# A two-layer hybrid backbone with routed experts: where a branch of the general path stands, and how rows and gates of the experts are made

## The chip, the cores and the metric

The kernel runs on one core of one Trainium2 chip. The time is the device time of one execution in microseconds (us). The core has five engines: TensorE (PE), VectorE (DVE), ScalarE (ACT), GpSimd (POOL) and SyncE (SP), each with its own stream of instructions, and 16 DMA engines that all queues share.

## The reference, cut to what matters

Two layers run over 256 latent tokens and 256 context tokens of width 1024. Each has an input projection, three groups of heads (retention, windowed and global attention), an output projection, and then a mixture of 16 experts of which each token uses two. The second layer needs only the latent tokens, so its experts see 256 rows, and those of the first see 512. Everything is f32.

```python
def _route(h, w_router, b_router):
    s = jax.nn.sigmoid(jnp.dot(h, w_router).astype(jnp.float32))
    ...
    w = jnp.take_along_axis(s, e_idx, axis=1)
    return e_idx, w / jnp.sum(w, axis=-1, keepdims=True)

def expert_block(args):
    xb, e = args
    a, u = jnp.split(xb @ w_gu[e], 2, axis=-1)
    return (jax.nn.silu(a) * u) @ w_down[e]

def reference(x, c, ctx, c_ctx, ada_w, ada_b, norm1, norm2, w_in, w_out, ret_decay, win_qk_gain, win_sink,
              glb_qk_gain, w_router, b_router, w_gate_up, w_down):
    for i in range(DEPTH):
        ...
        hx = _modulate(_rms(x, norm2[i]), sh2, s2).reshape(b * l, d)
        if last:
            x = x + g2 * _moe(hx, w_router, b_router, w_gate_up[i], w_down[i]).reshape(b, l, d)
        else:
            ...
            y = _moe(jnp.concatenate([hx, hc], 0), w_router, b_router, w_gate_up[i], w_down[i])
            x = x + g2 * y[:b * l].reshape(b, l, d)
            ctx = ctx + g2c * y[b * l:].reshape(ctx.shape)
    return x
```

`_modulate(h, shift, scale)` is h * (1 + scale) + shift. An expert has 8 MB of gate and up weights and 4 MB of down weights; two layers of 16 make 384 MB, which are read once.

## The kernel before, in words

**Stream of weights.** SP issues the weights in the order of their use as transfers of 1 MB into pages (`pump`, L164): per expert eight pieces of `w_gate_up` and four of `w_down`. A piece goes when a page is free; at most eight are in flight, since transfer n waits for the landing of transfer n - 8. In front of the experts the pages can be filled for expert 0 only, twelve pieces, because the experts run in an order that the routing finds (the fullest first): `order` holds it, and for each expert from 1 on SP loads its number from there into a register (`expert`, L144). The scheduler puts these loads together with the place where the code asks for them.

**Routing.** `route` turns the logits into probabilities, picks the two experts of each token, counts (a product with a triangular matrix, L1101 to L1106) and ranks the experts (L1120 to L1128, `order`). It works on small tiles of DVE, 30 or so instructions in a row. Meanwhile `rows` (L1013 to L1035) makes the normalized rows: factor and shift (L1016, L1017, L1019) and SP writes them to a buffer in DRAM, HX (L1020). In layer 1 it also cuts the rows into three bf16 parts `x3` (L1027 to L1035), on two pages of their own.

**An expert's rows.** `index` compares positions with a row of numbers: a one-hot matrix, in bf16, whose product with the token numbers (L1183) gives the row index of each slot; `gates` is a second product, of the same one-hot with the gates in three bf16 parts (L1194), which POOL has made (L1164 to L1169). In layer 0 POOL then gathers the rows from HX by an indirect transfer (L1213) and PE transposes them (`flip`, L1281). In layer 1 nothing is gathered: PE multiplies the rows' three parts with the one-hot (`place`, L1232, and L1249 in `pick_up`).

**An expert's products.** An expert with many tokens ("big": those with even numbers and 15 in layer 0; 0, 14 and 15 in layer 1) is computed as three products of high and low halves (L200 to L202); ACT makes the high half `hi` of each weight page (L190) and DVE the low one `lo` (L192), in five shared buffers. A small one (up to 64 tokens) multiplies in plain f32 (L1300, L1316). At an expert's end POOL scatters its result to DRAM (L1368). `between` puts the work on the next expert's rows between a running expert's pages.

**The general path.** If an expert gets more tokens than its slots hold, `overflow` (L1373) computes the rest in loops, behind a branch `tc.If(n > 0)` (L1388); with these inputs n is 0 and the branch jumps over it. All engines cross this branch. It stands in `moe` (L1436) just ahead of the first expert's rows, before the first weights behind expert 0's. Buffers that the general path uses too (those of `hi` and `lo`, lanes of the weight transfers) carry waits on both ways through the branch.

**What sets the order.** A scheduler orders the instructions of each engine by the order of the code and by dependencies; `issue_after` holds some work behind a named instruction.

Of the kernel before, what the change touches and what calls it, by code (L numbers as in the profile page):

```python
# [9 lines left out]
F32 = mybir.dt.float32  # L10
F32R = mybir.dt.float32r
BF = mybir.dt.bfloat16
# [9 lines left out]
NE = 16  # L22
# [38 lines left out]
class Kernel:  # L61
# [199 lines left out]
    def late_consts(self):  # L261
# [73 lines left out]
        self.tok = cp.tile([128, 4, 2], BF, name="tok")  # L335
        g.iota(self.tok[:, :, 0], pattern=[[128, 4]], base=-BIG, channel_multiplier=0, allow_small_or_imprecise_dtypes=True)
        g.iota(self.tok[:, :, 1], pattern=[[0, 4]], base=0, channel_multiplier=1, allow_small_or_imprecise_dtypes=True)
        self.tok2 = cp.tile([128, 4, 2], BF, name="tok2")
        v.tensor_scalar(self.tok2, self.tok, 2.0, None, op0=OP.mult)
# [568 lines left out]
    def out_proj(self, l):  # L908
# [27 lines left out]
        xr = [xg[t // 2][1][:, (t % 2) * 1024:(t % 2) * 1024 + 1024] for t in range(nt)]  # L936
        ss = self.tiny("ss2", [128, 4, 2])
# [51 lines left out]
        if nt == 4:  # L989
            mg.append(self.pgs.get("mods"))  # L990
            mb = mg[1][1]
            for r in range(2):
                self.modrow(mb[:, r * 1024:(r + 1) * 1024], l, r, 3, nc.gpsimd)
            self.spare += 1
            self.pump()
# [16 lines left out]
        def rows():  # L1012
            for t in range(nt):  # L1013
                b = mb[:, (t // 2) * 1024:(t // 2) * 1024 + 1024]
                if t % 2 and not l:
                    nc.scalar.activation(xr[t], xr[t], AF.Copy, scale=rs[:, t:t + 1])  # L1016
                    nc.gpsimd.tensor_tensor(xr[t], xr[t], b, op=OP.add)  # L1017
                else:
                    v.scalar_tensor_tensor(xr[t], xr[t], rs[:, t:t + 1], b, op0=OP.mult, op1=OP.add)  # L1019
                nc.sync.dma_start(self.HX[l][t * 128:(t + 1) * 128, :], xr[t])  # L1020
            if l:

                self.hx = [self.pgs.get("hx") for _ in range(2)]
                x3 = self.x3 = [self.hx[i // 2][1][:, (i % 2) * 1024:(i % 2) * 1024 + 1024].bitcast(BF).rearrange("p (t n) -> p t n", t=2)
                                for i in range(3)]
# [686 lines left out]
```

## Time and profile before

| | us |
|---|---|
| three runs | 1637.36, 1642.13, 1642.26 |
| median | 1642.13 |
| the profiled execution | 1637.78 |
| its span in the trace | 1635.5 |
| PE busy | 1443.6 (88%) |
| DVE busy | 884.2 (54%) |
| ACT busy | 612.8 (37%) |
| POOL busy | 200.6 (12%) |

The profile shows one execution, whose own time lies near the lowest of the three runs. Busy shares are means over very different stages: projections and attention, in which PE and DVE do small work and the transfer queues are half idle, the routing, in which nearly everything waits for a chain of small DVE instructions, and the experts, in which 384 MB go by. So the profile is read by windows of time, and in each window by what waits for what. Layer 0's routing lies at 331 to 361 us of the span, its experts behind it to some 800; layer 1's routing at 1099 to 1125, its experts to the end.

### The profile page before, as it was taken

What the parts mean: (1) busy time and instruction counts of PE and PEld (TensorE: products, weight loads), DVE (VectorE), ACT (ScalarE), POOL (GpSimd) and SP (SyncE); (2) the same over time, 40 slices, a digit from 0 to 9 for tenths busy, and PEclk for the clock granted to TensorE, in tenths of its full rate; (3) what the DMA queues carried; (4) which work ended last, traced back from release to release, by engine and by line L of the source; (5) the groups of instructions that cost most, each with busy time, mean ns of one, the idle gap of its engine ahead of it and who ended that gap; (6) DMA issues with size and microseconds to landing.
All of it is one profiled execution on the core that took longest, in us unless ns stands there. A gap on an engine that the chain in (4) does not pass through costs nothing. (4 is left out here: it accounts for less than half of the span.)

```text
span 1635.5 us, 21821 instructions
## 1 busy us (share of the span) xinstructions
PE 1443.6 (88%) x7890; PEld 864.6 (53%) x7890; DVE 884.2 (54%) x1648; ACT 612.8 (37%) x920; POOL 200.6 (12%) x216
## 2 busy tenths in 40 slices
PE   5999999929999999989888799976999888888888
PEld 4767756716664654645657667644433222222446
DVE  5776576476674654744779687967410000000577
ACT  3353404225563553643655554434300000000445
POOL 2000000440110110110033400021000000000030
PEclk9999999959999999999999999986999999999998
DMA  9763679538999999999997542743999999999993
GB/s 273 289 221 132 255 271 347 180 123 343 404 404 413 410 394 407 392 407 383 350 363 234 181 155 84 265 175 138 388 414 411 413 416 412 413 416 414 414 357 129
DMA packets 131099, 514.83 MB, mean 315 GB/s; under 512 B 14291, under 2 KB 40563, under 8 KB 92706
## 3 DMA queue, kind: packets, MB, share of 16 engines
q1 hardware_dynamic: 117536, 488.67, 76.3%
q0 software_dynamic: 8080, 16.60, 3.5%
q10 hardware_dynamic: 5362, 8.03, 1.5%
q8 instruction: 66, 1.08, 0.3%
q14 instruction: 55, 0.45, 0.1%
HBM read 503.24 MB, written 16.70 MB: 318 GB/s over the span
## 5 line engine op out<-in xcount | busy, mean ns | idle before, releaser
L192 DVE TENSOR_TENSOR lo<-w,hi 128x1024 fp32r<-128x1024 f32 x342 | 441.2, 1301 | 103.8 <-ACT hi L190 31.8
L190 ACT ACTIVATE hi<-w 128x1024 fp32r<-128x1024 f32 x344 | 359.4, 1059 | 179.9 <-PE gu L202 55.6
L1300 PE MATMUL gs<-w,ex 128*64 128x512 f32 x1280 | 298.9, 601 | 27.6 <-DMA w<-in_w_gate_up_dram 27.3
L1300 PEld LDWEIGHTS gs<-w,ex 128*64 128x64 f32 x1280 | 82.0, 136 | 196.5 <-issue 119.0
L201 PE MATMUL gu<-lo,ex 128*128 128x512 f32 (+1 forms) x384 | 155.7, 406 | 12.0 <-DVE lo L192 12.0
L1316 PE MATMUL ds<-w,ex 128*64 128x512 f32 x640 | 152.3, 603 | 7.9 <-DMA w<-in_w_down_dram 7.9
L202 PE MATMUL gu<-hi,ex 128*128 128x512 f32 (+1 forms) x384 | 153.5, 400 | 0.0
L200 PE MATMUL gu<-hi,ex 128*128 128x512 f32 (+1 forms) x384 | 134.5, 407 | 7.8 <-ACT hi L190 7.7
L1306 DVE TENSOR_TENSOR ex<-ex,gs 128x512 f32<-128x512 f32 x20 | 13.7, 687 | 214.6 <-PE gs L1300 214.6
L200 PE MATMUL px<-hi,hT 128*128 128x512 f32 (+1 forms) x304 | 114.6, 382 | 1.4 <-ACT hm L512 1.0
L201 PE MATMUL px<-lo,hT 128*128 128x512 f32 (+1 forms) x304 | 114.8, 378 | 0.4 <-DVE lo L192 0.4
L202 PE MATMUL px<-hi,hT 128*128 128x512 f32 (+1 forms) x304 | 114.3, 377 | 0.0
L1305 ACT ACTIVATE ex<-gs 128x512 f32<-128x512 f32 x20 | 11.9, 597 | 272.6 <-PE gs L1300 272.6
L1368 POOL DMA_INDIRECT y<-ex,ridx x28 | 43.7, 1561 | 568.5 <-ACT ex L1320 363.9
L201 PEld LDWEIGHTS gu<-lo,ex 128*128 128x128 f32 (+1 forms) x384 | 71.5, 186 | 39.5 <-DVE lo L192 21.5
L201 PE MATMUL dn<-lo,ex 128*128 128x512 f32 (+3 forms) x224 | 83.6, 374 | 5.6 <-DVE lo L192 5.6
L200 PEld LDWEIGHTS gu<-hi,ex 128*128 128x128 f32 (+1 forms) x384 | 70.4, 186 | 32.1 <-ACT hi L190 15.5
L1316 PEld LDWEIGHTS ds<-w,ex 128*64 128x64 f32 x640 | 40.0, 136 | 83.5 <-issue 56.8
L202 PE MATMUL dn<-hi,ex 128*128 128x512 f32 (+3 forms) x224 | 81.3, 364 | 0.0
L202 PEld LDWEIGHTS gu<-hi,ex 128*128 128x128 f32 (+1 forms) x384 | 71.5, 186 | 16.8 <-issue 0.2
L200 PE MATMUL dn<-hi,ex 128*128 128x512 f32 (+3 forms) x224 | 73.7, 370 | 0.0
L97 DVE COPY ex<-pl 128x512 f32<-128x512 f32 x12 | 8.3, 692 | 114.2 <-PE pl L1249 114.2
(344 smaller groups left out, 1945.1 us busy)
## 6 DMA issues: line engine op xcount, KB each, us to landing
w<-in_w_gate_up_dram SPq DMA_DIRECT2D x256, 1024.0 KB
w<-in_w_down_dram SPq DMA_DIRECT2D x128, 1024.0 KB
w<-in_ada_w_dram SPq DMA_DIRECT2D x40, 1024.0 KB
w<-in_w_in_dram SPq DMA_DIRECT2D x20, 1024.0 KB
w<-in_ada_w_dram SPq DMA_DIRECT2D x16, 512.0 KB
w<-in_w_out_dram SPq DMA_DIRECT2D x8, 1024.0 KB
y<-zero POOLq DMA_DIRECT2D x3, 1024.0 KB, 10.9
g<-modd ACTq DMA_DIRECT2D x6, 512.0 KB
```

What stands on the lines that cost most here:

```text
L97: nc.vector.tensor_copy(out, in_)
L190: nc.scalar.activation(hi, w, AF.Copy)
L192: (nc.gpsimd if after else nc.vector).tensor_tensor(lo, w, hi.bitcast(F32), op=OP.subtract)
L200: mm(o, a[0], b[0], start=first, stop=False)
L201: mm(o, a[0], b[1], start=False, stop=False)
L202: mm(o, a[1], b[0], start=False, stop=last)
L1300: nc.tensor.matmul(ps[n // 2][(n % 2) * 64:(n % 2) * 64 + 64], x[:, self.part(k)], t[:, n * 512:(n + 1) * 512], start=k == 0, stop=k == 7)
L1305: nc.scalar.activation(h, ps[0], AF.Silu)
L1306: nc.vector.tensor_tensor(h, h, ps[1], op=OP.mult)
L1316: nc.tensor.matmul(p[n * 64:n * 64 + 64], self.sx[2][:, self.part(ff)], t[:, f * 1024 + n * 512:f * 1024 + n * 512 + 512], start=ff == 0, ...
L1368: self.nc.gpsimd.indirect_dma_start(out=dst, out_offset=bass.IndirectOffsetOnAxis(ap=idx, axis=0), in_=y, in_offset=None, bounds_check=n - ...
```

## The change

Four things are changed together.

- `overflow(l)` is called behind `expert_down(l, 7)`, where it stood ahead of expert 0.
- One-hots are f32, and one product gives row index and gate (`ve` holds token number and gate side by side); `gates` and the three-part gates of POOL go. `arranged` sorts by one large multiplication on DVE, and gates come from DVE ahead of the ranking.
- In layer 1 the rows stay f32: `place` takes 16 f32 products where 48 bf16 ones stood, the two pages of parts are not taken, and the pages of the rows are kept to the end of the experts.
- In layer 0 HX is filled with the shift rows ahead of time by two transfers of 1 MB on ACT's queue, ACT scales the rows (four times), and POOL adds them into HX by accumulating transfers.

```diff
@@ norm and logits
+        if nt == 4:
+            for r in range(2):
+                nc.scalar.dma_start(self.HX[l][r * 256:(r + 1) * 256, :],
+                                    self.modd[l, r, 3 * 1024:4 * 1024].partition_broadcast(256))
...
         def rows():
             for t in range(nt):
-                b = mb[:, (t // 2) * 1024:(t // 2) * 1024 + 1024]
-                if t % 2 and not l:
+                if l:
+                    v.scalar_tensor_tensor(xr[t], xr[t], rs[:, t:t + 1], mb, op0=OP.mult, op1=OP.add)
+                    nc.sync.dma_start(self.HX[l][t * 128:(t + 1) * 128, :], xr[t])
+                else:
                     nc.scalar.activation(xr[t], xr[t], AF.Copy, scale=rs[:, t:t + 1])
-                    nc.gpsimd.tensor_tensor(xr[t], xr[t], b, op=OP.add)
-                else:
-                    v.scalar_tensor_tensor(xr[t], xr[t], rs[:, t:t + 1], b, op0=OP.mult, op1=OP.add)
-                nc.sync.dma_start(self.HX[l][t * 128:(t + 1) * 128, :], xr[t])
-            if l:
-                self.hx = [self.pgs.get("hx") for _ in range(2)]
...
-                for t in range(nt):
-                    nc.scalar.activation(x3[0][:, t], xr[t], AF.Copy)
-                for t, rest in enumerate((ma, mb)):
-                    nc.gpsimd.tensor_tensor(rest, xr[t], x3[0][:, t], op=OP.subtract)
-                    nc.scalar.activation(x3[1][:, t], rest, AF.Copy)
+                    nc.gpsimd.dma_start(self.HX[l][t * 128:(t + 1) * 128, :], xr[t], accum_op=OP.add)
...
@@ route
+        v.tensor_tensor(kw, s, sel, op=OP.mult)
+        v.tensor_reduce(gd, kw, axis=AX.X, op=OP.add)
+        v.reciprocal(gd, gd)
+        v.tensor_tensor(kx, kw, gd[:, :, None].to_broadcast([128, nt, 16]), op=OP.mult)
+        v.tensor_copy(ve[:, :, 0, 1], kx[:, :, 0])
...
-        def arranged(dst, src, e=v):
-            for t in range(nt):
...
-                e.tensor_tensor(m, perm, src[:, t, None, :].to_broadcast(b16), op=OP.mult)
-                v.tensor_reduce(dst[:, t], m, axis=AX.X, op=OP.add)
+        def arranged(dst, src):
...
+            v.tensor_tensor(m, perm[:, None].to_broadcast(o), src[:, :, None, :].to_broadcast(o), op=OP.mult)
+            v.tensor_reduce(dst, m, axis=AX.X, op=OP.add)
...
@@ index
         for t in range(nt):
-            nc.tensor.matmul(p[:, 0:2], oh[:, t], (self.tok2 if folded else self.tok)[:, t], start=t == 0, stop=t == nt - 1)
+            nc.tensor.matmul(p[:, 0:2], oh[:, t], ve[:, t], start=t == 0, stop=t == nt - 1)
+        self.placed = nc.vector.tensor_scalar(idx, p[:, 0:1], self.halfc[:S] if folded else float(BIG), None, op0=OP.add)
+        nc.vector.tensor_copy(gate, p[:, 1:2])
...
@@ place
-        for i in parts:
-            x = self.x3[i]
-            for t in range(nt):
-                for f in range(4):
+        for t in range(nt):
+            for f in range(4):
...
@@ moe
             self.expert_load(l, 0)
-            self.overflow(l)
...
             self.expert_down(l, e)
+            if e == NE // 2 - 1:
+                self.overflow(l)
```

How it moves instructions is seen at three places. The first is SP in front of layer 1's experts, from the read of `over1` to the first weight behind expert 0's (`w` is a weight page, `order1` the order of the experts, the row with eight waits the end of the jump). Before:

```order
L1377 TENSOR_LOAD over1_9940 [waits DVE_49]
L1388 COMPARE_AND_BRANCH
...
L1388 UNCONDITIONAL_BRANCH [waits DMAHW0_49,DMAHW1_49,DMAHW2_49,DMAHW3_49,DMAHW4_49,DMAHW5_49,DMAHW6_49,DMAHW7_49]
L1377 ISA x2
L164 ISA
L164 DMA w_10400<-in_w_gate_up_dram 128x2048 [waits DMAHW0_49,Activation_49]
L144 TENSOR_LOAD order1_9922
```

Eight loads of `order1` stand ahead of these rows. In the change, from the writes of HX on:

```order
L1020 DMA hx1_74<-xr_9511 128x1024 [waits DMAHW4_49,DVE_49]
L1020 DMA hx1_74<-xr_9511 128x1024 [waits DMAHW5_49,DVE_49]
L144 TENSOR_LOAD order1_9787 [waits DVE_49]
L144 ISA x2
L164 ISA
L164 DMA w_9844<-in_w_gate_up_dram 128x2048 [waits DMAHW6_49,Activation_49]
L164 ISA
L164 DMA w_9846<-in_w_gate_up_dram 128x2048 [waits DMAHW7_49]
L144 TENSOR_LOAD order1_9787
```

The branch is gone from this place, and the two transfers stand behind one load; seven others stand further back.

The second place is SP in layer 0 in the change, behind the last page of down weights ahead of the branch:

```order
L164 DMA w_5227<-in_w_down_dram 128x2x1024 [waits DMAHW4_49,PE_49]
L1357 TENSOR_LOAD over0_3129 [waits DVE_49]
L1368 COMPARE_AND_BRANCH
...
L1368 UNCONDITIONAL_BRANCH [waits DMAHW0_49,DMAHW1_49,DMAHW2_49,DMAHW3_49,DMAHW4_49,DMAHW5_49,DMAHW6_49,DMAHW7_49]
L1357 ISA x2
L144 TENSOR_LOAD order0_3111
L144 ISA x2
...
L164 ISA
L164 DMA w_5944<-in_w_gate_up_dram 128x2048 [waits DMAHW5_49,PE_49]
```

The row with eight waits stands where the jump ends; eight loads of `order0` follow it, of which two are shown, and then the stream goes on. Before, `w_down` was followed there by one load and the next transfer.

The third place is ACT in layer 0 at expert 8's down weights, before (`fl` are transposed rows of a later expert in PSUM, `gs` a small expert's product, `hi` the high half of a weight page):

```order
L1289 ACTIVATE ex_3992<-fl_6055 128x512 [waits PE_49]
L1289 ACTIVATE ex_3992<-fl_6080 128x512 [waits PE_49]
L1289 ACTIVATE ex_3144<-fl_6107 128x512 [waits PE_49]
L1320 ACTIVATE ex_3971<-ds_5989,rgate_3074 128x512 [waits DMASW4_49,PE_49]
L1289 ACTIVATE ex_3144<-fl_6120 128x512 [waits PE_49]
L1305 ACTIVATE ex_3971<-gs_6028 128x512 [waits DVE_49,PE_49]
L190 ACTIVATE hi_6137<-w_6004 128x1024 [waits DMAHW3_49,Activation_49]
```

In the change, from the end of the jump on:

```order
L1368 UNCONDITIONAL_BRANCH [waits Activation_49]
L190 ACTIVATE hi_6032<-w_5209 128x1024 [waits DMASW4_49,DMASW6_49,DMASW2_49,DMAHW0_49,DMASW0_49,DMAHW1_49,DVE_49,DMAHW4_49,PE_49,Activation_49]
L190 ACTIVATE hi_6042<-w_5209 128x1024 [waits DMAHW3_49,DMAHW5_49,DMAHW2_49,DMAHW6_49,DMAHW1_49,DMAHW7_49,DMASW1_49,Activation_49]
L190 ACTIVATE hi_6064<-w_5215 128x1024 [waits DMAHW6_49,DMAHW5_49,DMAHW2_49]
L1269 ACTIVATE ex_3242<-fl_5955 128x512 [waits PE_49]
L1269 ACTIVATE ex_3242<-fl_5974 128x512 [waits PE_49]
L1269 ACTIVATE ex_3132<-fl_6002 128x512 [waits PE_49]
```

The high halves of the down pages now stand ahead of the copies of `fl` and `gs`, and carry waits on many lanes.

## Rows read from the trace of the kernel before

**Rows 1.** Page, part 2: GB/s moved, 40 slices of 40.9 us.

```profile
GB/s 273 289 221 132 255 271 347 180 123 343 404 404 413 410 394 407 392 407 383 350 363 234 181 155 84 265 175 138 388 414 411 413 416 412 413 416 414 414 357 129
```

**Rows 2.** Windows: us, busy PE PEld DVE ACT POOL (count), PEclk, DMA share, GB/s.

```profile
333.00:342.00 9.00, 0.00 (x0) 0.00 (x0) 8.90 (x17) 2.41 (x3) 5.88 (x2) 0.50 0.57 233
344.00:348.00 4.00, 0.35 (x8) 0.19 (x4) 3.95 (x15) 0.00 (x0) 1.42 (x2) 0.50 0.00 0
360.00:364.00 4.00, 2.64 (x12) 2.15 (x12) 3.55 (x5) 2.32 (x3) 1.99 (x1) 0.50 0.61 205
635.00:760.00 125.00, 116.23 (x544) 70.35 (x541) 72.28 (x79) 60.88 (x67) 11.00 (x8) 1.00 1.00 392
1124.00:1128.00 4.00, 3.71 (x45) 2.83 (x43) 2.98 (x5) 2.95 (x3) 0.00 (x0) 0.50 0.44 147
1320.00:1380.00 60.00, 49.41 (x306) 15.72 (x303) 4.12 (x10) 3.54 (x6) 3.08 (x2) 1.00 1.02 414
```

**Rows 3.** Timeline, layer 0's routing: start, us, engine, line, work [idle before].

```profile
332.12 4.56 DVE L1019 SCALAR_TENSOR_TENSOR xr<-xr,n2r,mods 128x1024 f32<-128x1024 f32 x2
336.61 2.32 DVE L1060 TENSOR_SCALAR room<-room 128x64 f32<-128x64 f32 x1
346.56 1.12 POOL L1213 DMA_INDIRECT ex<-hx,ridx  x1 [1.98 <-DVE sq L1123]
347.93 0.16 DVE L1128 CAST order<-rod 128x16 int32<-128x16 f32 x1
358.71 1.09 PE L1281 MATMUL fl<-ident,ex 128*128 128x128 f32 x4 [13.27 <-PEq L1388]
361.47 1.20 PE L200 MATMUL gu<-hi,ex 128*128 128x512 f32 x2
360.25 0.98 SPq L164 DMA_DIRECT2D w<-in_w_gate_up_dram  x2
376.06 0.34 SPq L164 DMA_DIRECT2D w<-in_w_gate_up_dram  x1
```

**Rows 4.** Timeline, layer 1's routing, same columns.

```profile
1102.76 2.12 DVE L1062 TENSOR_TENSOR room<-room,brt 128x32 f32<-128x32 f32 x1
1104.92 2.03 DVE L1064 TENSOR_TENSOR room<-room 128x16 f32<-128x16 f32 x1
1114.58 0.16 DVE L1128 CAST order<-rod 128x16 int32<-128x16 f32 x1
1125.66 1.17 PE L200 MATMUL gu<-hi,ex 128*96 128x512 f32 x2 [0.29 <-ACT hi L190]
1125.00 0.36 SPq L164 DMA_DIRECT2D w<-in_w_gate_up_dram  x1
1132.25 0.35 SPq L164 DMA_DIRECT2D w<-in_w_gate_up_dram  x1
```

**Rows 5.** Lines L1388, L144: form, ns min/median/max, first and last start.

```profile
L1388 SPq EVENT_SEMAPHORE  x16: 17/17/17, 356.9 to 1124.4; - x16
L1388 PEldq COMPARE_BRANCH  x2: 3359/3748/4137, 354.2 to 1119.9; - x2
L144 SPq TENSOR_LOAD <-order x60: 261/270/470, 348.1 to 1589.6; - x60
```

**Rows 6.** Timeline, layer 0 around the end of expert 7.

```profile
634.69 3.80 SPq L164 DMA_DIRECT2D w<-in_w_down_dram  x1
648.62 1.06 ACT L190 ACTIVATE hi<-w 128x1024 fp32r<-128x1024 f32 x1 [0.71 <-DMA w<-in_w_down_dram]
```

**Rows 7.** Chain of waits in layer 1: start, us, what.

```profile
1156.77 1.87 PE gs L1300 x8
1162.98 1.51 PE pl L1249 x48
1353.34 20.06 DMA w<-in_w_down_dram
```

**Rows 8.** Part 6, DMA issues: what, queue, count, KB each, us to landing.

```profile
ex<-hx,ridx POOLq DMA_INDIRECT x16, 8.4
```

More of the change, by code (lines that the diff above doesn't have):

```diff
@@ L334, in late_consts @@
         v.memset(self.halfc[64:128], 2.0 * BIG + 1)
[L335 to L339, printed above, removed]
+        self.tok = cp.tile([128, 4], F32, name="tok")
+        g.iota(self.tok, pattern=[[128, 4]], base=-BIG, channel_multiplier=1, allow_small_or_imprecise_dtypes=True)
+        self.rowsof = cp.tile([128, 2, 16], F32, name="rowsof")
+        g.memset(self.rowsof, 2.0)
+        for l in range(2):
+            for e in BIG_AT[l]:
+                g.memset(self.rowsof[:, l, e:e + 1], 1.0)
     def ada_step(self, l, th, k):
@@ L1222, in expert_load, with place @@
             self.gather(l, self.xg[e % 2][:, 0:512], self.idx[:, e:e + 1], True)
-    def place(self, p, oh, b, parts=range(3)):
+    def place(self, p, oh, b):
         nt, S = oh.shape[1:]
-        for i in parts:
-            x = self.x3[i]
-            for t in range(nt):
-                for f in range(4):
-                    c = (b * 4 + f) * 128
-                    self.nc.tensor.matmul(p[:, f * S:(f + 1) * S], x[:, t, c:c + 128], oh[:, t],
-                                          start=i == t == f == 0, stop=i == 2 and t == nt - 1 and f == 3)
+        for t in range(nt):
+            for f in range(4):
+                c = (b * 4 + f) * 128
+                self.nc.tensor.matmul(p[:, f * S:(f + 1) * S], self.xr[t][:, c:c + 128], oh[:, t],
+                                      start=t == f == 0, stop=t == nt - 1 and f == 3)
     def pick_up(self, l, e, b):
@@ L1245, in pick_up @@
             nt = oh.shape[1]
-            for i in range(3):
-                for t in range(nt):
-                    for k in range(8):
-                        nc.tensor.matmul(p[:, self.part(k)], self.x3[i][:, t, k * 128:(k + 1) * 128], oh[:, t, 0:64],
-                                         start=i == t == k == 0, stop=i == 2 and t == nt - 1 and k == 7)
+            for t in range(nt):
+                for k in range(8):
+                    nc.tensor.matmul(p[:, self.part(k)], self.xr[t][:, k * 128:(k + 1) * 128], oh[:, t, 0:64],
+                                     start=t == k == 0, stop=t == nt - 1 and k == 7)
             return self.copy(self.sx[e % 2], p)
@@ L1461, in moe @@
             for b in range(2):
-                self.place(self.early[b], self.oh[0], b, (0, 1))
-            self.overflow(l)
+                self.place(self.early[b], self.oh[0], b)
             room()
-            pg.extend(self.hx)
+            pg.extend(self.rows)
             for b in range(2):
```

73 lines of the change are left out of this document (23 added, 50 removed).

## The prediction

> **What bounds the kernel now.** Read the slices of the transfer rate first: they say where the memory stream is the limit and where it stands still. Two plateaus of about 390 to 415 GB/s are the expert stages of the two layers [rows 1]. The windows then say how close the other engines are: in layer 0, 635 to 760 us, the queues are busy all the time (share 1.00) and PE for 116.2 of 125 us; in layer 1, 1320 to 1380, share 1.02 and PE 49.4 of 60 [rows 2]. So in layer 1 the stream alone sets the end: the chain of waits is made there of transfers of 20 us, which is one megabyte waiting its turn behind seven others [rows 7]. In layer 0 the stream leads and PE follows with 8.8 us of room. A microsecond in which no weight moves is lost in both.
>
> The stalls before the plateaus come next. In layer 0 the queues move 233 GB/s over 333 to 342 (the normalized rows on their way to DRAM, 2.1 MB), nothing in 344 to 348; weights start at 360.25 and run at half rate over 360 to 364 [rows 2, 3]. In layer 1 the first weight goes at 1125.00, the second at 1132.25 [rows 4]. What ends last in both stalls is the branch: after `order` is there (347.93, 1114.58) SP loads eight expert numbers, waits for `over`, crosses, and only then issues; PE crosses too (3.36 and 4.14 us in its compare) and starts its transposes at 358.71 with 13.27 us of idle put down to L1388 [rows 3 to 5].
>
> **The change part by part.** All terms are of the profiled execution, 1637.78 us (span 1635.5), which lies at the low end of the three runs; their median, 1642.13, is 4.35 above it.
>
> Front of layer 0. DVE no longer adds the shift: L1019 (4.56 us for two) goes, and L1060, which took 2.32 us beside POOL, should fall to the 0.2 of its neighbours. Against it stand some five small operations that come ahead (the gates), 0.2 each like L1128: about 1 us. So `order` and the gather's indices come 4.6 + 2.1 - 1 = 5.7 us sooner, `order` at 342.2 and the gather's issue, 346.56 before, at 341 [rows 3]. But the gather now waits for the four accumulating transfers. Plain writes of these 2.1 MB took the nine microseconds from 333 to 342 [rows 2]; no accumulating transfer is in the trace. From below it costs what the plain write does: landed at 342. From above it moves every byte twice, 2 x 9 us from 333: 351. I take 345, near the plain write, because the queues have nothing else to do and ACT hands over one row block after the other. The gather itself: 0.5 MB at 233 GB/s is 2.3 us and a transfer needs 1.8 us to start (below), so about 4 to 5; the median beside loaded queues is 8.4 [rows 8]. PE's transposes then start near 350 and not 358.71; no branch stands between. SP has its eight loads done by 342.2 + 5 = 347; its first four drops wait for the accumulations and for rooms, 349 to 351 and not 360.25. The next drops follow PE (376.06 now) [rows 3]. Gain **9.5 us**, between 2 (accumulations at 351, PE at 356) and 12.5.
>
> On this term by itself: the Trainium skill, "DMA: Bandwidth & Descriptors", section "Rules for kernel authors", says that an accumulating DMA reads its destination and writes it later, and that nothing holds the bytes in between. It gives no time; by it the upper end (each byte moved twice) would be the value, the gain some 3 and not 9.5, and the sum a loss of 0.8 us: the second rival below. No row here shows it.
>
> Front of layer 1. POOL's subtractions for the three parts go, and with them the stretch of L1062 and L1064 (2.12 and 2.03 us, to some 0.2 each): 3.8 us less, about 0.8 more for the gates, so `order` at 1111.6. SP then has one load, not eight, ahead of two weight transfers, at about 1112.3 and not 1125.00 (a thirteenth page is free, since the two pages of parts are not taken). PE waits for no branch and for no parts: its placing products are f32, 32 where 96 stood, and its first expert product comes near 1115 and not 1125.66 [rows 4]. The second drop of before, 1132.25, follows PE's first pages, so it comes 10.7 to 12.7 sooner, and the additional page is worth up to 2.5 more (20.06 us over eight in flight [rows 7]). Gain **13 us**, between 10 and 15.3.
>
> Branch in layer 1, behind expert 7. SP's row at the join waits for every weight lane, where before nothing was in flight. So the stream runs dry, then SP passes eight semaphores and, as the order shows, eight loads of `order` before the next transfer. Before, from its first semaphore (356.9) to its first transfer (360.25) it took 3.35 us with four loads; the load alone is 0.27, with its checks 0.6 by that difference; four more make 5.6 [rows 3, 5]. From an issue to full rate: 205 GB/s over 360 to 364 is half of the plateau, so 1.8 us [rows 2]. Loss **7.4 us**, 6 to 10, with nothing to hide it: PE has 10.6 us of room in 60, the stream none [rows 2].
>
> Branch in layer 0. The same 7.4 for the stream. Besides, ACT's first work behind the branch is `hi` of a down page, which waits for SP to be through, with the copies out of PSUM behind it. SP issued its last transfer ahead of that place at 634.69; 20.06 us later it lands, so SP is through at about 655.5 [rows 6, 7]. PE gets four pages of expert 9 done (1.87 us each) after 4 us of branch, to 646, and then stands until ACT moves, 656 to 657, 10 to 11 us, where `hi` started at 648.62 before [rows 5 to 7]. The stream stands for 7.4 of that anyway; the remaining 3 to 4 fit into the 8.8 us that PE has [rows 2]. Loss **8.4 us**: 7.4 and one for what doesn't fit; 7.4 to 12.5. POOL's scatter of expert 7 must also land there; the next gather behind it isn't due for a dozen microseconds.
>
> With one answer each: the index product in f32, and two copies where a reduction stood, lie on PE and DVE beside the stream; placing a small expert takes 48 products in 1.51 us now [rows 7] and 16 f32 ones that I put at 0.1 to 0.2 each, 1.6 to 3.2: hidden by PE's room in layer 1, up to 1.5 us at the tail. The 2 MB that prefill HX go out in slices at 120 to 180 GB/s [rows 1]: hidden, and 5 us if the cover were gone. Together **+1**.
>
> Sum: 9.5 + 13 - 8.4 - 7.4 - 1 = 5.7 us gained: 1632.1 beside the profiled 1637.78, and 1636.4 beside the median.
>
> **The rivals.** *More stays:* the front of layer 0 gives PE's whole 12, the thirteenth page all its 2.5 (15.3), and both branches cost the stream alone: 27.3 - 14.8 = 12.5, 1629.6. For it: every one of these is what PE's own start gives; against it, that all hold at once. If the join did not drain the stream at all (the change not doing what the order shows), the losses would go too: about 1620.
>
> *The front is late:* accumulations land at 350 or after, PE starts at 355; layer 0 gives 3, the rest as summed: 3 + 13 - 16.8, so 1643. For it: POOL issues them, and nothing in the trace prices them.
>
> *The stop costs more than the stream's gap,* and the change is slower. The place is layer 0 behind expert 7. PE's crossing took 3.36 to 4.14 us with empty queues; beside full ones a gather takes 8.4 and not 4 to 5, so 6 to 7. After a standstill of PE the granted clock was 0.50, its lower level of 1.2 GHz, as in 1124 to 1128 [rows 2], so its first pages take twice as long: 3 to 4 us. PE then stands or crawls for 11 + 3 + 4 = 18 us; from 7.4 + 8.8 = 16.2 on it costs more than the stream's gap, and with page releases late besides I put it at 14; layer 1, by the same crossing and clock, at 10. With fronts of 8 and 11 that is 19 - 25 = 6 us lost: 1648. Against it: the crossing runs while the stream still empties.
>
> On this by itself: the Trainium skill, "Runtime: NRT & Kernel Launch", section "Instruction fetch mechanics", has a taken branch out of the current window fetch its target by DMA before the engine goes on, which speaks against a branch amid a full stream. The trace agrees as far as it goes, with 3.36 and 4.14 us on PE [rows 5]; none of its crossings is beside full queues.
>
> **How the numbers follow.** The forecast 0.42, more stays 0.16, no drain 0.04, front late 0.20, slower 0.18. A measurement of this kernel tells 0.3%, 4.9 us, from no change. The forecast's own spread is 1630 to 1642: 0.28 of its chance is beyond that bound, 0.12 within, 0.02 slower; more stays and no drain are faster; front late is within for 0.17 and faster for 0.03. So faster 0.51, same 0.29, slower 0.20. The range goes from 1625, which leaves out the lowest ends, to the slower rival's 1648.
>
> **What would show it.** In the profile after: the first weight of layer 0 at 349 to 351, of layer 1 near 1112 less what came before; PE's first expert product 9 to 12 us sooner in both; behind expert 7 one gap of 6 to 9 us in the transfer rate in each layer, with eight loads of `order` in it, and in layer 0 a stop of PE of some 10 us that ends with ACT's `hi`. Wrong would be: no gap, a gap over 12, PE waiting for the gather beyond 355, or the experts of layer 0 ending later by more than the gap.

## The result: 0.65% slower

| | us |
|---|---|
| before, median of 5 runs (1637.36 to 1642.26) | 1640.59 |
| after, median of 5 runs (1648.05 to 1653.70) | 1651.17 |
| after / before | 1.0065, 95% interval [1.0044, 1.0086] |
| profiled execution of after, its span | 1653.70, 1651.7 |

The prediction was 1636, between 1625 and 1648, with "faster" as the likeliest. The change is slower by 10.6 us in the medians and by 15.9 between the two profiled executions, since that of before lies at the low end of its runs and that of after at the top. So the account below, made on the profiles, holds some 5 us too much that belong to no step.

Read the account first. It is worked out from both traces: by how much later the n-th weight transfer, counted from 0, has landed in after. A transfer moves in 16 parts and has landed when the last of them has.

| place | transfers | later than before, us |
|---|---|---|
| layer 0, experts 1 to 7 | 16 to 104 | -2.5 to +1.9, -0.1 at 104 |
| layer 0, behind the branch, in its later experts | 120 to 184 | 6.4 and 7.3 at 120 and 128, 11.6 and 10.2 at 176 and 184 |
| layer 0, its last one | 191 | 12.5 |
| layer 1, the last ones ahead of its routing | 192, 200 | 14.0, 13.6 |
| layer 1, first ones behind its routing | 204, 208 | 0.0, -0.7 |
| layer 1, up to the branch | 232 to 296 | 4.8 to 6.0 |
| layer 1, behind the branch, last transfer | 312 to 376, 383 | 16.8 to 15.3, 17.3 |

So: front of layer 0 nothing, its branch about 12.5 lost, attention 1.5 lost, front of layer 1 some 14 gained, 6 of them given back within the first experts, its branch about 10.5 lost: 0 + 12.5 + 1.5 - 14 + 6 + 10.5 = 16.5, beside 17.3 at the last transfer and 16.2 in the spans.

**The branches.** The page of after, transfer rate in 40 slices of 41.3 us (it answers [rows 1], which is the same view of the kernel before; so with the views below): the slices that begin at 619 and 1404 us, 298 and 302, are the two branches. The plateaus are as high as before.

```profile
GB/s 274 291 218 176 252 279 336 149 155 339 399 410 412 409 397 298 373 412 408 338 390 215 188 166 78 250 170 229 370 414 408 416 416 410 302 415 414 414 347 153
```

Windows of after around both (answers [rows 2]; us, busy PE PEld DVE ACT POOL with counts, granted clock, DMA share, GB/s):

```profile
640.00:645.00 5.00, 5.00 (x24) 1.53 (x20) 0.00 (x0) 0.00 (x0) 0.00 (x0) 1.00 1.01 352
645.00:650.00 5.00, 0.00 (x1) 0.00 (x0) 0.00 (x0) 0.00 (x0) 0.00 (x0) 0.94 0.54 216
650.00:655.00 5.00, 0.00 (x0) 0.00 (x0) 0.00 (x0) 0.00 (x0) 0.00 (x0) 0.50 0.38 155
655.00:660.00 5.00, 0.00 (x0) 0.00 (x0) 1.20 (x2) 2.29 (x3) 0.00 (x0) 0.50 0.05 22
660.00:665.00 5.00, 3.08 (x10) 1.49 (x12) 2.54 (x4) 1.74 (x3) 0.00 (x0) 0.50 0.16 36
665.00:670.00 5.00, 5.00 (x26) 1.89 (x22) 0.88 (x3) 0.00 (x0) 1.34 (x1) 0.86 0.99 418
...
1405.00:1410.00 5.00, 5.00 (x35) 3.27 (x36) 1.02 (x2) 0.00 (x0) 0.00 (x0) 1.00 0.90 365
1410.00:1415.00 5.00, 5.00 (x26) 1.72 (x24) 0.69 (x1) 0.60 (x1) 0.00 (x0) 1.00 0.11 47
1415.00:1420.00 5.00, 4.66 (x22) 1.29 (x18) 0.00 (x0) 0.69 (x1) 0.99 (x1) 1.00 0.00 2
1420.00:1425.00 5.00, 0.73 (x2) 0.29 (x4) 0.00 (x0) 0.00 (x0) 0.55 (x1) 0.92 0.87 312
```

What the six windows of layer 0 moved, 1199 x 5 us, takes 14.6 us at 410 GB/s: 15.4 us of transfer are missing. The four of layer 1 moved 726 x 5, 8.8 us at 414: 11.2 are missing. In layer 0 the rate does not fall off a cliff: 216 and 155 GB/s for ten microseconds, with a share of 0.54 and 0.38 of the DMA engines, before it is near nothing.

Where the slope comes from stands in the landings, and it stood in the trace of before. The 16 parts of a transfer drift apart while the stream runs full: in before they ended 1.4 us apart at layer 0's first transfers (median of 16 to 39) and 12.6 at 104 to 115; in layer 1 2.4 at 212 to 249 and 5.5 at 300 to 308. The last transfer ahead of the branch ended over 13.1 us in layer 0 of after (644.4 to 657.6) and 6.6 in layer 1 (1407.3 to 1413.8). The join waits for the last part, and behind it the spread is small again, 0.8 us in after (median of 116 to 129).

Lines L1368 and L144 of after (answers [rows 5]; ns min/median/max, first and last start), and the timeline around the end of expert 7 in layer 0 (answers [rows 6]; start, us, engine, line, work, idle before and what ended it):

```profile
L1368 SPq EVENT_SEMAPHORE  x16: 17/17/17, 647.5 to 1413.9; - x16
L1368 PEldq COMPARE_BRANCH  x2: 6147/6238/6328, 630.5 to 1383.8; - x2
L144 SPq TENSOR_LOAD <-order x60: 262/269/462, 352.2 to 1610.0; - x60
```

```profile
629.27 9.08 SPq L164 DMA_DIRECT2D w<-in_w_down_dram  x4
637.18 3.65 PE L1280 MATMUL gs<-w,ex 128*64 128x512 f32 x16 [2.79 <-PEq L1368]
657.71 2.95 ACT L190 ACTIVATE hi<-w 128x1024 fp32r<-128x1024 f32 x3 [22.59 <-SPq L1368]
658.80 2.36 DVE L192 TENSOR_TENSOR lo<-w,hi 128x1024 fp32r<-128x1024 f32 x2 [30.49 <-ACT hi L190]
661.92 1.12 PE L1261 MATMUL fl<-ident,ex 128*128 128x128 f32 x4 [16.92 <-DVE ex L1270]
662.89 0.96 SPq L164 DMA_DIRECT2D w<-in_w_gate_up_dram  x2
```

SP waits at the join until 657.7, which is what frees ACT; then come its eight loads, 5.2 us, and the next transfer at 662.89. PE has nothing from 645 to 661.92, 16.92 us, and resumes at the lower clock, 0.50. What that does to experts, by POOL's scatter at the end of experts 7, 8 and 13, before and then after:

```profile
634.67 1.57 POOL L1368 DMA_INDIRECT y<-ex,ridx  x1 [3.70 <-ACT ex L1320]
664.47 1.58 POOL L1368 DMA_INDIRECT y<-ex,ridx  x1 [8.37 <-ACT ex L1362]
830.98 1.55 POOL L1368 DMA_INDIRECT y<-ex,ridx  x1 [30.10 <-DMA w<-in_w_gate_up_dram]
```

```profile
635.40 1.57 POOL L1348 DMA_INDIRECT y<-ex,ridx  x1 [28.53 <-ACT ex L1300]
686.65 1.58 POOL L1348 DMA_INDIRECT y<-ex,ridx  x1 [17.19 <-ACT ex L1342]
842.73 1.56 POOL L1348 DMA_INDIRECT y<-ex,ridx  x1 [29.99 <-DMA w<-in_w_gate_up_dram]
```

Level (+0.7) at expert 7, 22.2 late at expert 8, 11.8 at expert 13: PE gave 10 back by its room and not more. This lateness sets the end of layer 0: PE is then busy nearly all the time (89.5 of 90 us from 690 to 780), and SP waits for pages that DVE and PE have still to read, 84 us from 665 to 840 beside 32 for landings, where in before it was 52 and 84 (640 to 830). So the transfers, just behind the branch 4 to 6 us later than ahead of it, end the layer as late as PE.

**The front of layer 0.** Timeline of after (answers [rows 3]):

```profile
334.66 3.21 ACT L1022 ACTIVATE xr<-xr,n2r 128x1024 f32<-128x1024 f32 x3
338.17 0.86 POOL L1023 DMA_DIRECT2D hx<-xr  x1 [0.18 <-issue]
339.18 0.20 ACT L1050 ACTIVATE warm<-room 128x1 f32<-128x1 f32 x1
339.42 0.20 DVE L1055 TENSOR_SCALAR room<-room 128x64 f32<-128x64 f32 x1 [5.34 <-ACT warm L1050]
346.10 1.84 PE L1174 MATMUL idx<-rve,oh 128*128 128x2 f32 x8 [1.34 <-DVE oh L1170]
355.63 1.09 PE L1261 MATMUL fl<-ident,ex 128*128 128x128 f32 x4 [7.69 <-DMA ex<-hx,ridx]
357.41 1.22 PE L200 MATMUL gu<-hi,ex 128*128 128x512 f32 x2 [0.69 <-ACT ex L1269]
360.17 0.22 DVE L1175 TENSOR_SCALAR ridx<-idx,halfc 128x1 int32<-128x1 f32 x1 [1.79 <-PE idx L1174]
360.51 1.64 SPq L164 DMA_DIRECT2D w<-in_w_gate_up_dram  x3
```

DVE's chain starts at 339.42 and not 336.61. `room` is changed in place and `warm` reads it; `warm` now stands behind ACT's scalings, so DVE waits 5.34 us for it. The accumulating transfers were issued from 334.92 on and, by their records, landed at 340.2, 345.1, 347.6 and 350.1; windows 340 to 348 show 181 and 180 GB/s at shares of 0.98 and 0.91, where plain writes ran at 233 [rows 2]. PE's first expert product comes at 357.41, 4 us sooner than the 361.47 of [rows 3], yet the first transfer at 360.51 is level with 360.25: it and DVE's first `lo` at 360.43 stand behind `ridx`, the row index of expert 1. For the transfer the code asks for this in both kernels (`self.hold = self.placed`, then `add_manual_dep` in `pump`), and in all 14 traces it starts 0.02 to 0.13 us after that `ridx` ends. Of SP's waits in after (us in total, times, longest) the longest of this kind, 3.4 us, is here:

```profile
SPq L164 <- DVE ridx L1175: 13.1, 5, 3.4
```

In before it was

```profile
359.93 0.28 DVE L1186 TENSOR_SCALAR ridx<-idx,halfc 128x1 int32<-128x1 f32 x1 [5.81 <-PE idx L1183]
```

which ended at 360.21, when SP was just through with its loads (360.19): two waits ended together there. In after the index product in front of it starts 1.2 us sooner (358.43 for 359.59) and takes 1.70 us where 0.29 stood, behind PE's first expert product. So of PE's 4 us 0.8 are left at the first product with `lo` (361.70 for 362.47), and nothing is left behind the next index product, 0.95 us for 0.25. From there on the transfers follow PE as before.

**The front of layer 1.** Timeline of after (answers [rows 4]); layer 1's attention ends 13.9 us later than before and the chain of the routing starts 13.2 later, so 13.2 is to be taken off each start:

```profile
1124.04 0.16 DVE L1131 CAST order<-rod 128x16 int32<-128x16 f32 x1
1125.03 10.72 SPq L164 DMA_DIRECT2D w<-in_w_gate_up_dram  x3
1127.52 0.67 PE L200 MATMUL gu<-hi,ex 128*96 128x512 f32 x2
```

`order` is 3.7 us sooner, the first transfer 13.2 and PE's first expert product 11.3. Then PE is full and the stream is not. Two windows of after, and under them the same stretch of before, in which PE is full too and the stream is nearer to its plateau:

```profile
1150.00:1190.00 40.00, 40.00 (x206) 22.86 (x207) 16.89 (x20) 13.84 (x17) 0.53 (x1) 1.00 0.88 347
1190.00:1216.00 26.00, 26.00 (x138) 11.21 (x136) 2.00 (x5) 1.88 (x3) 1.49 (x2) 1.00 0.99 395
```

```profile
1150.00:1180.00 30.00, 30.00 (x179) 14.64 (x180) 13.34 (x17) 10.07 (x12) 0.00 (x0) 1.00 0.98 384
1180.00:1216.00 36.00, 36.00 (x254) 13.53 (x252) 3.61 (x9) 2.52 (x5) 3.17 (x2) 1.00 1.02 411
```

### The profile page after: what moved, and what is told of

It is laid out like the page before. It is cut to its first block, busy times and chain, and to the rows that moved or that the text cites. A ratio compares the mean times of both kernels' runs of the same rounds, so it can differ in the third digit from the quotient of the medians.

```text
span 1651.7 us, 21312 instructions
## 1 busy us (share of the span) xinstructions
PE 1491.6 (90%) x7634; PEld 925.4 (56%) x7634; DVE 869.4 (53%) x1637; ACT 610.8 (37%) x918; POOL 186.3 (11%) x210
## 5 line engine op out<-in xcount | busy, mean ns | idle before, releaser
L1280 PEld LDWEIGHTS gs<-w,ex 128*64 128x64 f32 x1280 | 87.0, 139 | 175.7 <-issue 153.4
L201 PE MATMUL gu<-lo,ex 128*128 128x512 f32 (+1 forms) x384 | 157.2, 409 | 10.7 <-DVE lo L192 10.3
L1296 PE MATMUL ds<-w,ex 128*64 128x512 f32 x640 | 147.3, 599 | 1.5 <-DMA w<-in_w_down_dram 1.5
L1175 DVE TENSOR_SCALAR ridx<-idx,halfc 128x1 int32<-128x1 f32 x20 | 4.4, 218 | 131.7 <-PE idx L1174 131.7
## 6 DMA issues: line engine op xcount, KB each, us to landing
y<-zero POOLq DMA_DIRECT2D x3, 1024.0 KB, 10.5
```

The source lines that it names most:

```text
L201: mm(o, a[0], b[1], start=False, stop=False)
L1175: self.placed = nc.vector.tensor_scalar(idx, p[:, 0:1], self.halfc[:S] if folded else float(BIG), None, op0=OP.add)
L1280: nc.tensor.matmul(ps[n // 2][(n % 2) * 64:(n % 2) * 64 + 64], x[:, self.part(k)], t[:, n * 512:(n + 1) * 512], start=k == 0, stop=k == 7)
L1296: nc.tensor.matmul(p[n * 64:n * 64 + 64], self.sx[2][:, self.part(ff)], t[:, f * 1024 + n * 512:f * 1024 + n * 512 + 512], start=ff == 0, ...
```

## The experiments

Theory after the result: the slower rival. A stop in the middle of a full stream costs more than one in front of it. Rivals: the f32 products, the accumulating transfers, or the moved `warm` carry the loss. Each median stands with its ratio to the kernel before on the same chip. That kernel had medians of 1637.9 to 1638.5 there, and 1640.59 in the comparison with after; so a difference to after is given twice, by medians and by ratios. A median is of 4 to 12 executions, of 4 in the runs of one branch moved or doubled, of the plain rows and of the mixed version.

**The branch left out of both kernels.**

```diff
-            if e == NE // 2 - 1:
-                self.overflow(l)
```

> The changed kernel with the general path and its branch left out of both layers (the part for experts over capacity is not computed; with these inputs nothing depends on it). Theory: the two branches in the stream cost the change most, 11 to 12 us each, because the weight stream is drained at the join and its DMA engines run dry up to 13 us apart; expected about 1629 us (1651 less 22), the steps of +14 and +12 us in the lag of landed weights gone. Rival: the branch is nearly hidden and the loss comes from accumulating transfers and f32 products; then it stays at 1645 or above.

1633.64 us, 0.9980 [0.9964, 0.9997]. Without its branches the changed kernel is 17.5 us faster by medians, 14 by ratios (0.0085 of 1638): the theory in kind, 5 to 8 less than it asked. The rest of the change, with no branch to pay anywhere, leaves 4.4 us against the kernel before, which pays its own.

```diff
             self.expert_load(l, 0)
-            self.overflow(l)
...
```

> The kernel before with the general path and its branch left out of both layers. It prices the branch where it stood, in the fronts. Theory: layer 0's first product is held by the branch for some 7 us after the gather has landed, layer 1's for 6 to 8 us; expected 1626 us (1640 less 14). Rival: the fronts are held by routing and gather alone, the branch is worth under 5 us in both; then 1635 or above.

1631.54 us, 0.9954 [0.9939, 0.9968]. In front the branches cost 6.5 us in all (7.5 by the ratio), between the two expectations, and by landings all of it lies in layer 1 (8.2 sooner at its first transfers, of which some 2 are given back; 0 in layer 0). In the kernel before this is the most that moving the branch could bring. And it is 2.1 us less than the changed kernel without branches (4.3 by ratios): with the branch away from both, the rest of the change brings nothing. The trace says why layer 0 gives nothing. Its timeline, in which all is 5.2 us late from the first weights on:

```profile
357.86 1.22 PE L200 MATMUL gu<-hi,ex 128*128 128x512 f32 x2 [0.69 <-ACT ex L1289]
359.21 0.80 DVE L1179 TENSOR_TENSOR oh<-iota,rpr 128x512 bf16<-128x512 bf16 x1
361.41 1.54 POOL L1213 DMA_INDIRECT ex<-hx,ridx  x1 [0.50 <-DVE ridx L1186]
369.22 0.45 PE L1271 MATMUL tu<-ident,ex 128*128 128x128 f32 x1 [4.19 <-DMA ex<-hx,ridx]
371.83 1.06 ACT L190 ACTIVATE hi<-w 128x1024 fp32r<-128x1024 f32 x1 [6.14 <-PE gu L202]
```

PE's first product is 8.8 us sooner than in before, after the 5.2 are taken off. But behind two pages of expert 0 PE's queue has the transposes of expert 1, and these wait for a gather whose indices stand at the end of DVE's sorting chain. PE waits 4.19 us for the rows, ACT 6.14 for PE, pages come free late, and the gain is gone. The waits say so; no run took this gather away. (In before and in after these transposes stand later in PE's queue, at 380.6 and 380.7, and PE doesn't wait for them.)

**Only the branch moved, in the kernel before** (both calls of `overflow` ahead of expert 0 go).

```diff
+            if e == NE // 2 - 1:
+                self.overflow(l)
```

> The kernel before with one part of the change alone: the branch moved behind expert 7 in both layers. Theory: fronts gain 14, drains cost 22 to 24: 1648 to 1650 us, slower than before. Rival (move is good, other parts are at fault): 1630 or below.

1656.84 us, 1.0109 [1.0079, 1.0139]: above the theory's range, and slower than the whole change by 5.7 (7 by ratios). So the place of the branch is enough for a loss. Beside the kernel with no branch, 1631.54, the two crossings cost 25.3 here. Its windows in layer 0 show the same slope, and PE's compare the same length:

```profile
645.00:650.00 5.00, 0.00 (x0) 0.00 (x0) 0.00 (x0) 0.00 (x0) 0.00 (x0) 0.85 0.74 300
650.00:655.00 5.00, 0.00 (x0) 0.00 (x0) 0.00 (x0) 0.00 (x0) 0.00 (x0) 0.50 0.42 168
655.00:660.00 5.00, 0.00 (x0) 0.00 (x0) 0.00 (x0) 0.00 (x0) 0.00 (x0) 0.50 0.13 52
```

```profile
L1388 PEldq COMPARE_BRANCH  x2: 6157/6272/6388, 628.4 to 1385.3; - x2
```

**The branch back in front, the rest of the change kept** (`overflow` ahead of expert 0 again in both layers).

```diff
             self.expert_load(l, 0)
+            self.overflow(l)
...
```

> The changed kernel with one part undone: the branch back in front of the experts, all else kept. Theory: the drains go (-22), the fronts pay the branch again (8 in layer 1, 4 to 8 in layer 0): 1641 to 1645 us, about the kernel before. Rival: if f32 products and accumulating transfers are at fault, 1655 or above.

1646.23 us, 1.0054 [1.0035, 1.0074]: 4.9 less than after by medians, 1.8 by ratios, with intervals that overlap. So in the changed kernel the crossings cost 12.6 in front (1646.23 less 1633.64), and 14 to 17.5 behind expert 7; in the kernel before 6.5 and 25.3. The direction is the theory's both times, the size depends on the rest. Against before, the rest of the change costs 8 with the branch in front: by landings of its profiled execution, which was its fastest (1641.56), 4 to 6 in layer 0's front, where accumulations and branch both stand ahead of PE's start, and 4.5 given back of 6.9 gained in layer 1's.

**Layer 0's rows as before** (plain writes, shift added by DVE and POOL, `warm` ahead of them; the rest as changed).

```diff
-                    nc.gpsimd.dma_start(self.HX[l][t * 128:(t + 1) * 128, :], xr[t], accum_op=OP.add)
...
+                    nc.sync.dma_start(self.HX[l][t * 128:(t + 1) * 128, :], xr[t])
...
-        rows()
...
+        rows()
```

> The changed kernel with one part undone: layer 0's rows get their shift on DVE and POOL again and go out by plain writes, and the activation that reads the probabilities (its table load) stands ahead of the rows; the branch stays behind expert 7. Theory: layer 0's front is held by the chain for expert 1's rows (its one-hot, index product and gather), so undoing the accumulation moves the front by less than 3 us: 1648 to 1654 us. Rival: the accumulating transfers, landed at 350, hold the front; then the first expert product comes 5 us or more sooner and the time is 1646 or less.

1645.52 us, 1.0054 [1.0035, 1.0073] beside after's [1.0044, 1.0086]: the intervals overlap. The time lies in the rival's range and the trace in the theory's. PE has the gather's rows at 353.69 and its first product starts at 355.46, 2 us sooner than in after, and the first new transfer at 358.46, also 2 sooner. So accumulating and `warm` cost about 2 us together by the trace and by the ratios (1.8); the 5.6 of the medians can't be told from that.

**A second pair of branches behind expert 11.**

```diff
-            if e == NE // 2 - 1:
+            if e in (NE // 2 - 1, NE - 5):
```

> The changed kernel with the suspected cost doubled: the general path and its branch stand behind expert 7 and once more behind expert 11 (it isn't entered with these inputs). Theory: each crossing in the stream costs 9 to 12 us of landed weights, so 18 to 24 more in all: 1669 to 1675 us. Rival (a crossing costs only the 7.4 us of SP's loads and restart): 1665 or less.

1682.10 us, 1.0265 [1.0248, 1.0282]: 31 more than after (33 by ratios) for two more crossings, above the theory's 18 to 24. One more costs 15.5, about twice what one of the first two costs; by landings, beside after, the second one of layer 0 takes 16 (10.0 to 26.2 between transfers 160 and 168) of which 5 have come back by the layer's end, that of layer 1 and the tail behind it some 15; the profiled execution was 10.7 later already ahead of its first branch. A crossing in the stream is a loss every time; why the 16 was not settled.

**Layer 1's branch of before at the very end of the stream.**

```diff
                 self.place(self.early[b], self.oh[0], b, (0, 1))
-            self.overflow(l)
...
+            if e == NE - 3 and last:
+                self.overflow(l)
```

> The kernel before with layer 1's branch moved behind expert 13, where few weights are left to come; layer 0's stays in front. Theory: layer 1's front gives 8 of which 2 to 3 go to pages, 5 to 6 us net; the late crossing stops PE, which is the bound there, for its 4 to 6 us and for the drain: between 1634 and 1645, near the kernel before. Rival (the late crossing is hidden as little as the one behind expert 7): 1642 to 1646.

1646.83 us, 1.0064 [1.0045, 1.0082]. By landings layer 1's front gains 7, and the crossing behind expert 13 costs 14: near its end the stream hides no more of it than in its middle. The time lies just above both ranges.

**The mixed version**: plain rows, layer 0's branch in front, layer 1's behind expert 13, products in f32.

```diff
             self.expert_load(l, 0)
+            self.overflow(l)
...
-            if e == NE // 2 - 1:
+            if e == NE - 3 and last:
                 self.overflow(l)
```

> Layer 0's rows and branch as before, f32 products and one product for row and gate as in the change, layer 1's branch behind expert 13. Theory: layer 0 costs 2 to 4 more than before by its f32 index products, layer 1's front gives 16 less 7 for f32 placing, the late crossing takes 4 to 10 back: 1632 to 1642 us. Rival (f32 products cost nothing): under 1632.

1652.71 us, 1.0098 [1.0078, 1.0118]: missed, by 14 again at the late crossing, with 5 lost in the front of layer 0 (7.4 later at transfer 24, 1.9 at transfer 8).

**The branch in front, reached sooner.** `over` is computed ahead of `order`, and `order` is cast behind the branch, so that SP's loads of it stand behind the crossing.

```diff
             self.overflow(l)
+            self.ordered(l)
```

> A version meant to beat both: the kernel before, branch in front in both layers, but the count of tokens over capacity is made on DVE ahead of the experts' order, and the order is handed to SP behind it, so that the engines cross while the rows are still being placed, and SP crosses ahead of six of its eight loads. Theory: the front of layer 1 costs 8 by the branch, of which 4 to 5 are won; layer 0's front is held by expert 1's rows and gives nothing: 1633 to 1635 us. Rival (SP's crossing holds ACT as before): 1637 to 1639.

On the kernel before: 1637.76 us, 1.0003 [0.9991, 1.0014], in the rival's range. Its profile shows the 3 us in layer 1, first transfer and first product in its timeline:

```profile
1121.59 10.33 SPq L164 DMA_DIRECT2D w<-in_w_gate_up_dram  x3
1122.52 1.17 PE L200 MATMUL gu<-hi,ex 128*96 128x512 f32 x2 [1.87 <-ACT hi L190]
```

3.4 and 3.1 us sooner than in [rows 4], and the landings keep 3 to the end; the median has nothing of it. One execution shows the gain, twelve together do not: whatever the branch in front holds up, 3 us less of it can't be measured as time.

> The same early count and late order, on the changed kernel with plain rows in layer 0 and the branch in front in both layers: f32 placing in layer 1, no three parts. Theory: layer 1's front gives 11 to 13 against before, f32 placing takes 6 to 7 of it, layer 0 loses 0 to 3: 1632 to 1637 us. Rival (f32 placing costs all that the front gives): 1639 or above.

On the kernel with plain rows and f32 products, the branch in front: 1639.64 us, 1.0015 [1.0002, 1.0029]. Missed, in the rival's range; by landings it loses 3 to 5 in layer 0, gains 8.3 in layer 1's front, gives 3.5 of them back and ends 1.3 later than before. No version with the general path in it beats the kernel before.

**Half of the placing**, beside the same kernel with all of it. What is placed is the first 128 of 256 rows.

```diff
-            for t in range(nt):
-                for k in range(8):
-                    nc.tensor.matmul(p[:, self.part(k)], self.xr[t][:, k * 128:(k + 1) * 128], oh[:, t, 0:64],
...
+            for k in range(8):
+                nc.tensor.matmul(p[:, self.part(k)], self.xr[0][:, k * 128:(k + 1) * 128], oh[:, 0, 0:64],
...
```

> The changed kernel without the general path, and of the placing of the small experts of layer 1 only the first 128 of 256 rows: 8 products in f32 for an expert and not 16 (the other half of the rows is left out). Placing a small expert took 4.0 us with 16 products, so 2.0 are expected, near the 1.51 of the three bf16 parts. Theory (the f32 placing gives back 5.5 us of layer 1's front, since PE has nothing to spare over 1130 to 1216): some 4 to 6 us less than the same kernel with all 16, so 1628 to 1630 where that had 1633.6; the lag of the landings grows by under 2 us between 1130 and 1216. Rival (what is given back goes to pages, the high and low halves, or the queues, and the placing only fills PE's room): within 1.5 us of the kernel with all 16, and the lag grows by 5 as there.

> The changed kernel without the general path once more, as the control of the run with half the placing on the same chip: 1631 to 1636 by either theory (1633.64 before).

1633.06 us, 0.9961 [0.9946, 0.9976] with half, 1634.39, 0.9981 [0.9969, 0.9992] with all: 1.3 us between the medians, 3.3 by the ratios, where the theory had 4 to 6 and the rival up to 1.5. By landings the front of layer 1 gives back 2.3 us with half and 6.0 with all (mean lag of transfers 206 to 211 against 240 to 291; what is gained is that of 192 to 203 less that of 206 to 211). The other traces order themselves by the same measure. The kernel before without branches, with them behind expert 7, and with layer 1's behind expert 13 place in bf16 and give back 1.7, 1.9 and 1.4 of 7.0 gained; the changed kernel with the branch in front gains 6.9 as well and gives back 4.5, its version with the early count 3.5 of 8.3; the other versions with full f32 placing and layer 1's branch out of its front, after among them, gain 13 to 16 and give back 5.6 to 6.3. So f32 placing is the larger part of what is given back, 2 to 4 us, and some 2 go back without it.

## Why the prediction was wrong, step by step

By runs the sum splits in two. The steps that failed are the two gains of the fronts: the wait behind the branch in layer 0, and the room that was to hide the placing in layer 1. The branches behind expert 7 were put at 15.8 and cost 14 to 17.5. Everything else was put at 21.5 gained and gives 4.4 without branches, 4.1 when that was run again. So it is the fronts that failed, by 17 us.

**Front of layer 0, 9.5 predicted, about 0 measured.** Two things failed. The sizes: the accumulations landed at 350.1, beside the upper end of 351 and not the 345 taken; the index product took 1.84 us in f32 where it was put at nothing; DVE's chain started 2.8 us later, behind `warm`, where it was to be sooner, which the order of ACT's instructions would have told, and `order` came at 351.96 and not at 342.2. And the logic: the first drops were put behind "the accumulations and for rooms", at 349 to 351, but the code ties the first of them to expert 1's row index, which ended at 360.39 (360.21 before). "The next drops follow PE" was right, but what PE and DVE wait for next was not looked for. In after that is expert 1's index again: the f32 product delays `ridx` and with it `lo`, and the 4 us of PE's start are gone. In the kernel before without its branches it is expert 1's gather at the end of DVE's sorting chain (8.8 us sooner, 0 gained). Both readings are of waits in the traces.

On the accumulation by itself: the Trainium skill, "DMA: Bandwidth & Descriptors", section "Rules for kernel authors", has such a transfer read its destination and write it later. The trace agrees: four transfers of 0.5 MB, to 350.1, with 180 GB/s at shares of 0.91 to 0.98, where plain writes were done at 342 with 233 GB/s at a share of 0.57; for each byte the DMA engines were busy about twice as long.

**Front of layer 1, 13 predicted, 13.2 to 13.9 measured, 6 of it given back.** The parts were right: one load ahead of the transfer, no crossing, no parts. What failed is the sentence that PE's room hides the placing. A small expert's placing measured, in the chain of waits of after (answers [rows 7]):

```profile
1403.78 3.72 PE pl L1230 x32
```

32 instructions, two for each product, in 3.72 us, where the bound was 1.6 to 3.2 and bf16 took 1.51. PE has room on the plateau; just behind the front it has none, 40 of 40 and 26 of 26 us busy from 1150 to 1216, with the stream at 347 and 395 GB/s. With half of the products 2.3 us went back and not 6.0, with bf16 ones 1.4 to 1.9, so placing is the larger part of it; the remainder has no proof.

**The branches.** Their sum was right and its working was not. By the windows the stream lacks 15.4 and 11.2, where 7.4 was put for each. The times of the stop were near: SP through the join at 657.7 for 655.5, eight loads in 5.2 us, PE's stop 16.9 for 10 to 11. But the working let the stream run at its full rate until the last byte lands. In fact nothing refills the queues that are done: from 645 to 657.7 some 1.9 MB went by, which at 410 GB/s is 4.7 us of 12.7. Those 8 us had no term. The term was to be had: it is the spread of a transfer's parts, 12 to 13 us in layer 0 of before. By landings the stop is smaller at first, 4 to 6 us behind the branch of layer 0 and 10 in layer 1; in layer 0 PE's lateness, 22 us at expert 8 where 10 to 11 were put for its stop, makes it 12.5 by the end. That the kernel without branches is only 14 to 17.5 faster, and not 23 to 27, has two reasons in the traces: executions spread by 5 us and more (the profiles, 1653.70 and 1628.43, differ by 25), and without the stop other limits take part, as the 6 given back in layer 1. How much each is was not settled.

**The rivals.** The slower one came nearest in time, 1648. It had the place right, and its reason in layer 0, PE that stands and crawls; by landings its 14 and 10 for the branches are near 12.5 and 10.5, though the runs without branches give 14 to 17.5 for both. Its fronts were wrong, 8 and 11 where 0 and 8 came (14 less 6), so its time is luck in part. The rival of the late front had the accumulations at 350 and PE at 355 right (350.1 and 355.6), and still 3 us too many for them. Of the signs of being wrong two came: a gap over 12, by the windows in layer 0, and PE waiting for the gather beyond 355 (to 355.5). PE's compare beside full queues, 6.15 to 6.33 us, lies in the 6 to 7 of the slower rival. In each of the 22 crossings of all runs one packet of 16 KB on instruction queue q8 moves inside the compare: it starts 0.9 to 1.0 us behind the compare's start in front of the experts and 3.5 to 3.9 beside the full stream, and the compare ends 1.3 to 1.5 us behind the packet. So it is this packet that comes late; that it brings PE's instructions is inferred.

On this by itself: the Trainium skill, "Runtime: NRT & Kernel Launch", section "Instruction fetch mechanics", has a taken branch whose target lies out of the window in hand fetch it by DMA before the engine goes on. The traces agree for PE: the packet of 16 KB, and 6.15 to 6.33 us beside full queues, 3.36 to 4.14 beside empty ones [rows 5].

**What was lacking** is a ceiling. The branch in front costs 6.5 us in the kernel before, all of it in layer 1; one run with it left out says so. The prediction credited the two fronts with 22.5 from the waits that ended last there, and each of these had another behind it.

**Open.** The 1.5 us in attention; the 2 us that layer 1 gives back without f32 placing; why two crossings cost 25.3 in the kernel before and 14 to 17.5 in the changed one; the 16 us of the second crossing in layer 0.

## What to carry to other kernels

A join that waits for every transfer in flight belongs where the stream stands still anyway; price it by the tail in which the queues run out one after the other, the loads behind it and the restart, not by the gap between the last landing and the next issue. The tail can be read ahead of time from how far apart the parts of one transfer end in the running stream. And before the removal of a stall is credited, follow the next waits of the engine that starts sooner, and the dependencies that the code itself sets: here they took all of layer 0's gain.

## What the runs showed of the hardware that was not expected

- The queues needed some 13 us to run empty out of a full stream: 352, 216, 155, 22 GB/s in steps of 5 us. The 16 parts of one transfer of 1 MB ended between 644.4 and 657.6. This spread grows while the stream runs full, from 1.4 us to 12.6 within some 90 transfers in layer 0 of before, and the stop in after sets it back to 0.8.
- f32 products with two columns cost nearly as much as those with 64: 255 ns for one instruction beside 279, two for each product. The 96 index products in f32 kept PE for 26.6 us, 192 in bf16 (index and gates) for 14.8 by their rows. The four products of layer 0's first index took 1.84 us at the lower clock, 0.27 for as many in bf16.
- A jump over a skipped region took PE 3.3 to 4.1 us beside idle queues (ten crossings in six kernels) and 6.0 to 6.4 beside full ones (twelve crossings in six); in the second case one packet of 16 KB on the instruction queue starts 2.5 to 2.9 us later.
